# Three buffers for a head's keys and values, two for the padded projections, in a bidirectional gated DeltaNet and GLA layer

## The chip, the cores and the metric

The kernel runs on one core of a Trainium2 chip. The metric is the time of one execution on the device in microseconds (us), median of the runs.

## The reference

One encoder layer on x of 1024 tokens by 1024 channels, in fp32. The input is normalised and goes through one projection; two branches read its columns, and their gated sum goes through an output projection.

```python
h = rmsnorm(x, ln_pre_w)
proj = h @ w_in
...
qkv_a = silu(centred_depthwise_conv(qkv_a, conv_w))          # 5 taps
q_a, k_a = l2norm(q), l2norm(k)                              # 8 heads of 128
o_a = gated_delta_rule(q_a, k_a, v_a, lg_f, beta_f) + flip(gated_delta_rule(flipped, lg_b, beta_b))
y_a = (rmsnorm(o_a, gdn_norm_w) * silu(z_a)) @ w_proj_gdn
y_b = ...                                                    # gated linear attention, 4 heads
merged = sigmoid(gate_a) * y_a + sigmoid(gate_b) * y_b
out = x + rmsnorm(merged @ w_out, ln_post_w)
```

The delta rule is S_t = a_t S_(t-1) (I - b_t k_t k_t^T) + b_t v_t k_t^T, o_t = S_t q_t, for each head and each direction. The reference works by chunks, with a triangular solve in each chunk, and the state goes from chunk to chunk.

## The kernel before

All products of the projections are split: an operand is the sum of two parts of lower precision, and three products of 512 columns (hh·hi, hl·hi, hh·lo) make one of full precision. A projection of 128 output channels (`project`, L256) is 48 products of 512 columns on TensorE (PE), called pj in the rows; its weights come by DMA and are cut into parts by ScalarE (ACT, hi), GpSimd (POOL) or VectorE (DVE, lo).

The delta rule ("GDN") goes head by head, each in three parts that overlap with the neighbours'.

**gdn_project(h)** (L497) makes k, q and v of a head, in this order, and z. Each of k, q, v is projected, evacuated by ACT (L504) into a padded tile xp, whose edges POOL clears (L502), and convolved with five taps over 1024 tokens: the first by DVE (L516; for q by ACT, L514), the others as four `scalar_tensor_tensor` on DVE (L518). The results are the tiles a0 (q), a1 (k), a2 (v), two buffers each, so that head h+1's k takes the place of head h-1's. The four SiLUs of a head (L499), with that of z of the head before, are put together, since ACT loads a table for them and another one to go back (L309, L311).

**gdn_inverse(h)** (L589) works on chunks of 128 tokens, 8 for each direction. PE transposes k (L600), ACT copies it and takes squares (L601, L605) and a logarithm (L613), and makes the decays dt by 16 exponentials (L622). PE multiplies k with itself (L630), DVE makes um of it (L633), and 120 small operations of DVE solve the triangular systems of 32 rows (L655 and L657, tiles tmp and yl). From xq (L665) on, PE and DVE and ACT build larger inverses in turns (L686 to L725), v is transposed and scaled (L733, L734), and q is multiplied with k (L740, L743).

**gdn_scan(h)** (L746) carries the states S of both directions through 8 steps. In each, for both directions: S times k (L781, PE), r (L783, DVE), um times r (L786, PE), vd (L789, DVE) and vn (L791, ACT) from it, kt (ktok times vd, L796, PE), S (L801, DVE) and the outputs po (L770, PE). r reads k by the product and v directly; so the buffers of k and v of head h come free with the end of scan h. After the scan come squares (L816, L817), the norm (L483, L488), and o (L125, L475).

The tile scheduler writes the instruction order of each engine by priorities, the lowest first among what is ready by its own model, which counts the waits for buffers. Scan h (P_HEAD*(h+1)+P_Z) and inverse h (P_HEAD*(h+1)+P_Y) stand ahead of everything with P_FILL: the next head's gdn_project and the gate projections, pj_t (13 of them at head 7), fill what is left. At head 7 stand also `gla_stacks` (L541, tiles r0, r0l), which prepare the second branch.

In `scan_gates` (L401), once at the start, two constant masks are loaded: stl (a tag of its own, 1 KiB in each partition) and mid (tag t2, shared with many small tiles).

Of the kernel before, what the change touches and what calls it, by code (L numbers as in the profile page):

```python
# [8 lines left out]
F32 = mybir.dt.float32  # L9
# [4 lines left out]
P = 128  # L14
T = 1024
# [39 lines left out]
CONSTS = {}  # L55
# [33 lines left out]
def layer_kernel(  # L89
# [6 lines left out]
    nc = tc.nc  # L96
# [16 lines left out]
    @contextmanager  # L113
    def at(priority):

        before = tc.cur_priority
        tc.cur_priority = priority
        yield
        tc.cur_priority = before

    def bank(pool, tag, name):
        return pool.tile([P, 512], F32, tag=tag, name=name)
# [133 lines left out]
    def project(name, evac, src=None):  # L256

        ps = [bank(pj, "pj", f"pj_{name}_{th}") for th in range(2)]
        for g in range(2):
            hi, lo = next_w(name, g)  # L260
            for th in range(2):
                piece(ps[th], hi, lo, src or (hh, hl), th, g, KH)
        for th in range(2):
            evac(th, ps[th])
# [11 lines left out]
    def project_out(name, dst):  # L276


        def evac(th, ps):
            for c in range(2):  # L280
                g_ = gpool.tile([P, 256], F32, tag="gt", name=f"g{name}_{th}_{c}")
                nc.scalar.copy(g_, ps[:, 256 * c:256 * c + 256])  # L282
                nc.sync.dma_start(dst[:, half(th)][:, 256 * c:256 * c + 256], g_)

        project(name, evac)
# [9 lines left out]
    o_c, _ = CONSTS["cf"]  # L295
# [12 lines left out]
    def table(n):  # L308
        tc.keep_in_program_order(nc.scalar.add_instruction(mybir.InstLoadActFuncSet(  # L309
            name=nc.get_next_instruction_name(), engine=mybir.EngineType.Activation, ins=[], outs=[],  # L310
            act_func_set_id=n)))  # L311

    def exp_ln_table():

        table(EXP_LN)
# [85 lines left out]
    def scan_gates(pool):  # L401
# [6 lines left out]
            nc.scalar.dma_start(alog[:, d, :], al.broadcast_to([P, HA]))  # L408
            nc.scalar.dma_start(dtb[:, d, :], dt.broadcast_to([P, HA]))
        smT = pool.tile([64, T], F32, tag="osq", name="smT", bufs=1)  # L410
        stl = pool.tile([P, 2, P], F32, tag="stl", name="stl", bufs=1)
        nc.scalar.dma_start(stl, consts[:, CONSTS["su"][0]:CONSTS["su"][0] + 2 * P].rearrange("p (d i) -> p d i", d=2))
        mid = pool.tile([P, 2, 130], F32, tag="t2", name="mid", bufs=4)
        nc.scalar.dma_start(mid, consts[:, o_c:o_c + 260].rearrange("p (d i) -> p d i", d=2))
        strict = [stl[:, d] for d in range(2)]
        ones = part(tb_, 3, 1)
        nc.gpsimd.memset(ones, 1.0)
        for th in range(2):
# [26 lines left out]
        psg = bank(pg, "g", "psg")  # L445

        for d in range(2):
            rhs = lg[:, d].rearrange("p h n -> p (h n)")
            for q, m in enumerate((mask[d], strict[d], ones)):
                o = (d * 3 + q) * 64  # L450
                nc.tensor.matmul(psg[:, o:o + 64], lhsT=m, rhs=rhs, start=True, stop=True)

            o = 384 + d * 64
            nc.tensor.matmul(psg[:, o:o + 64], lhsT=mid[:, d, :P], rhs=rhs, start=True, stop=True)
        nc.scalar.activation(ev, psg[:, :384].rearrange("p (d q h n) -> p d q h n", d=2, q=3, h=HA), AF.Exp)
        nc.vector.tensor_scalar(nE, ev[:, :, 0], -1.0, None, op0=ALU.mult)
        cm = part(ta_, 0, 1)
# [37 lines left out]
    H64 = (slice(0, 64), slice(64, 128))  # L495

    def gdn_project(h, pool):  # L497
        a = [pool.tile([P, T], F32, tag=f"a{j}", name=f"{'qkv'[j]}{h}", bufs=2) for j in range(3)]
        silu = lambda t: tc.keep_in_program_order(nc.scalar.activation(t, t, AF.Silu))  # L499
        for j in A_ORDER:  # L500
            xp = pool.tile([P, T + 4], F32, tag="xp", name=f"xp{j}_{h}", bufs=XP)
            nc.gpsimd.memset(xp[:, 0:2], 0.0)  # L502
            nc.gpsimd.memset(xp[:, T + 2:T + 4], 0.0)
            evac = lambda th, ps: nc.scalar.copy(xp[:, 2 + th * 512:2 + th * 512 + 512], ps)  # L504
            if h == 0 and j == A_ORDER[0]:
                evac(0, ps_a[0])
                for i in range(2, 4):
                    a_steps[i]()
                evac(1, ps_a[1])
            else:  # L510
                project(f"a{j}_{h}", evac)
            ct = j * 8 + h
            if j == 0:
                nc.scalar.mul(a[j], xp[:, 0:T], cw[:, ct, 0:1])  # L514
            else:
                nc.vector.tensor_scalar(a[j], xp[:, 0:T], cw[:, ct, 0:1], None, op0=ALU.mult)  # L516
            for k in range(1, 5):
                nc.vector.scalar_tensor_tensor(a[j], xp[:, k:k + T], cw[:, ct, k:k + 1], a[j], op0=ALU.mult, op1=ALU.add)  # L518
            if h == 0 and j == A_ORDER[0]:
                table(SILU)  # L520
                silu(a[j])
                exp_ln_table()
        if h == 0:
            table(SILU)
            for j in A_ORDER[1:]:
                silu(a[j])
            exp_ln_table()
            with at(P_FILL):
                project_out("z0", z_d[:, 0])
            return a  # L530
        project_out(f"z{h}", z_d[:, h])
        zs[h - 1] = gdn_z(h - 1, pool)
        table(SILU)
        for t in a + [zs[h - 1]]:
            silu(t)
        exp_ln_table()
        return a
# [33 lines left out]
    def gdn_z(h, pool):  # L571
        z = pool.tile([P, T], F32, tag="zs", name=f"zs{h}", bufs=1)
        nc.sync.dma_start(z, z_d[:, h])
        return z
# [246 lines left out]
    with tc.tile_pool(name="gdn", bufs=1) as pool, tc.tile_pool(name="gdns", bufs=2) as sm:  # L821
        scan_gates(pool)
        o128 = mconst.tile([P, P], F32, name="o128")
        nc.gpsimd.memset(o128, 1.0 / 128)
        with at(P_HEAD):
            dt = gdn_decay(0, pool)
        qkv = gdn_project(0, pool)
        for h in range(HA):
            with at(P_HEAD * (h + 1) + P_Y):
                inv = gdn_inverse(h, pool, sm, qkv, dt)  # L830
            if h < HA - 1:
                with at(P_HEAD * (h + 1) + P_DT):
                    dt = gdn_decay(h + 1, pool)
            cur = qkv
            with at(P_FILL + P_HEAD * (h + 1)):
                if h < HA - 1:
                    qkv = gdn_project(h + 1, pool)
            with at(P_FILL + P_HEAD * (h + 1)):
                gates(("gdn", h))
            if h == HA - 1:  # L840
                with at(P_HEAD * (h + 1) + P_Z - 1000):
                    gla_stacks(pool)
            with at(P_HEAD * (h + 1) + P_Z):
                gdn_scan(h, pool, sm, cur, *inv)
# [311 lines left out]
```

## Time and profile before

| | |
|---|---|
| Median of three runs | 1640.31 us (1637.06 to 1645.77) |
| The profiled execution | 1647.96 us, of it the span 1646.2 us |
| TensorE busy | 1538.3 us, 93% of the span |
| VectorE busy | 871.7 us, 53% |
| ScalarE busy | 704.3 us, 43% |
| GpSimd busy | 190.5 us, 12% |
| Mean granted clock of TensorE | 0.958 of full speed |

The busy times are sums over the whole span. The eight heads of the delta rule take the time from about 40 to 850 us, some 90 us for each; the second branch and the output projection take the rest, in which TensorE is nearly always busy. The clock is the share of the full 2.4 GHz that the chip granted; a dip means stretches at the lower level of 1.2 GHz.

### The profile page before, as it was taken

The numbers are of one execution on the slowest core, as the hardware profiler recorded it, in microseconds if no ns is written. First come the engines' busy times: TensorE is split into PE (matmuls) and PEld (weight loads), VectorE is DVE, ScalarE is ACT, GpSimd is POOL, SyncE is SP. The second block draws the span as 40 slices with busy tenths as digits, with TensorE's granted clock in tenths as the row PEclk, the third lists the DMA queues.
The fourth block names the chain that finished last, engine by engine and source line by source line (L and its number), as shares of the span: only waits on it lengthen the run. The fifth ranks groups of instructions, "written<-read, shape, count | busy, mean of one in ns | idle before, by whom it ended". The sixth has DMA issues, their size and how long they took to land.

```text
span 1646.2 us, 24982 instructions
## 1 busy us (share of the span) xinstructions
PE 1538.3 (93%) x9500; PEld 1295.8 (79%) x9500; DVE 871.7 (53%) x2252; ACT 704.3 (43%) x1488; POOL 190.5 (12%) x207
## 2 busy tenths in 40 slices
PE   6988978998998999899899999999999999999998
PEld 6867866777787878787677888898898988787887
DVE  5485485877879696878531012323314336445413
ACT  5452454436363635554332233535425545423311
POOL 3220111111213011110000020010120100000000
PEclk9996987999898999999999999999999999999999
DMA  5320221131212113131233322131131234755414
GB/s 160 126 68 18 80 71 33 33 106 36 96 46 90 46 33 116 50 99 48 77 121 100 103 65 64 27 103 33 55 85 48 80 100 143 238 157 173 128 45 154
DMA packets 142435, 142.07 MB, mean 86 GB/s; under 512 B 11419, under 2 KB 115403, under 8 KB 141285
## 3 DMA queue, kind: packets, MB, share of 16 engines
q1 hardware_dynamic: 134546, 126.11, 25.6%
q10 hardware_dynamic: 7128, 12.26, 2.4%
q0 software_dynamic: 640, 2.10, 0.4%
q8 instruction: 75, 1.23, 0.3%
q14 instruction: 46, 0.38, 0.1%
HBM read 109.98 MB, written 30.46 MB: 85 GB/s over the span
## 4 chain that ended last, share of the span: by engine, by line
PE 64%; DVE 16%; ACT 11%; DMA 5%; issue 3%; SPq 0%; POOL 0%; ACTq 0%; DVEq 0%; POOLq 0%
PE pj_t L252 8%; PE pj_y L252 7%; PE pj_v L241 6%; PE pout L141 5%; PE pj_g L252 5%; DVE yl L657 4%; PE pj_a L252 4%; DVE tmp L655 4%; PE pj_z L252 4%; PE pj_k L252 3%; PE pj_q L252 2%; ACT dt L622 2%; PE po L770 2%; PE psb L948 2%; PE pob L970 2%
## 5 line engine op out<-in xcount | busy, mean ns | idle before, releaser
L252 PE MATMUL pj_a<-hh,hi_a 128*128 128x512 f32 x368 | 153.6, 417 | 16.5 <-ACT xp L504 9.4
L252 PE MATMUL pj_a<-hl,hi_a 128*128 128x512 f32 x368 | 152.6, 415 | 0.0
L252 PE MATMUL pj_a<-hh,lo_a 128*128 128x512 f32 x368 | 152.1, 413 | 0.0
L252 PE MATMUL pj_t<-hh,hi_t 128*128 128x512 f32 x256 | 103.9, 406 | 2.8 <-ACT gt L282 2.8
L252 PE MATMUL pj_t<-hh,lo_t 128*128 128x512 f32 x256 | 104.2, 407 | 0.0
L252 PE MATMUL pj_t<-hl,hi_t 128*128 128x512 f32 x256 | 103.7, 405 | 0.0
L182 POOL TENSOR_TENSOR lo_a<-raw_a,hi_a 128x512 fp32r<-128x512 f32 x48 | 63.8, 1329 | 311.0 <-ACT hi_a L178 257.0
L252 PEld LDWEIGHTS pj_a<-hh,hi_a 128*128 128x128 f32 x368 | 73.0, 198 | 31.6 <-ACT xp L504 10.2
L657 DVE TENSOR_TENSOR yl<-yl,tmp 128x54 f32<-128x54 f32 (+13 forms) x480 | 96.3, 241 | 0.1
L655 DVE TENSOR_TENSOR tmp<-ulb,yl 128x54 f32<-128x54 f32 (+13 forms) x480 | 90.4, 228 | 0.1
L252 PEld LDWEIGHTS pj_a<-hl,hi_a 128*128 128x128 f32 x368 | 72.4, 197 | 13.9 <-issue 0.7
L252 PEld LDWEIGHTS pj_a<-hh,lo_a 128*128 128x128 f32 x368 | 72.4, 197 | 13.7 <-issue 0.8
L252 PE MATMUL pj_y<-ob,hi_y 128*128 128x512 f32 x256 | 79.1, 390 | 0.9 <-DVE gb L1075 0.9
L141 PE MATMUL pout<-wo,hh 128*128 128x512 f32 (+1 forms) x272 | 79.7, 377 | 0.0
L791 ACT COPY vn<-psc 128x128 f32<-128x128 f32 x128 | 32.2, 265 | 108.5 <-DVE vd L789 72.1
L241 PE MATMUL pj_v<-lo_v,hh 128*128 128x256 f32 x256 | 72.5, 283 | 0.0
L241 PE MATMUL pj_v<-hi_v,hl 128*128 128x256 f32 x256 | 72.5, 283 | 0.0
L241 PE MATMUL pj_v<-hi_v,hh 128*128 128x256 f32 x256 | 72.5, 283 | 0.0
L796 PE MATMUL psc<-vd,ktok 128*128 128x128 f32 x224 | 45.4, 304 | 24.8 <-ACT vn L791 24.7
L182 POOL TENSOR_TENSOR lo_v<-raw_v,hi_v 128x512 fp32r<-128x512 f32 x32 | 41.3, 1290 | 233.1 <-ACT hi_v L178 229.0
L796 PEld LDWEIGHTS psc<-vd,ktok 128*128 128x128 f32 x224 | 34.7, 198 | 39.5 <-ACT vn L791 37.7
L184 DVE TENSOR_TENSOR lo_t<-raw_t,hi_t 128x512 fp32r<-128x512 f32 x32 | 22.0, 689 | 71.7 <-ACT hi_t L178 71.7
(315 smaller groups left out, 4024.2 us busy)
## 6 DMA issues: line engine op xcount, KB each, us to landing
raw_a<-in_w_in_dram SPq DMA_DIRECT2D x48, 256.0 KB
dt<-cr_d SPq DMA_DIRECT2D x8, 1024.0 KB
qe<-eg_d SPq DMA_DIRECT2D x16, 512.0 KB
raw_t<-in_w_in_dram SPq DMA_DIRECT2D x32, 256.0 KB
gt_d<-gt SPq DMA_DIRECT2D x64, 128.0 KB
raw_v<-in_w_in_dram SPq DMA_DIRECT2D x32, 256.0 KB
xt<-in_x_dram SPq DMA_DIRECT2D x8, 512.0 KB
raw_z<-in_w_in_dram SPq DMA_DIRECT2D x16, 256.0 KB
```

The source lines that it names most:

```text
L141: nc.tensor.matmul(ps, lhsT=a(k), rhs=b(k), start=(s == 0), stop=(s == len(steps) - 1))
L182: nc.gpsimd.tensor_tensor(lo, raw, hi.bitcast(F32), op=ALU.subtract)
L241: nc.tensor.matmul(ps[b][:, c * 256:(c + 1) * 256], lhsT=a[th][:, kk, ts], rhs=w[:, k, :], start=kk == 0 and i == 0 and c == 0, stop=kk == ...
L252: nc.tensor.matmul(ps[:, cols], lhsT=a[:, k, :], rhs=b[th][:, kk, cols], start=kk == 0 and a is hi and b is src[0], stop=kk == KD - 1 and ...
L622: nc.scalar.activation(dt[:, u], dt[:, u], AF.Exp, bias=bias[:, d, n:n + 1])
L655: nc.vector.tensor_tensor(tv, ul2[:, i, 0:i].unsqueeze(2).broadcast_to([P, i, w_]), yv[:, i].unsqueeze(1).broadcast_to([P, i, w_]), op=ALU ...
L657: nc.vector.tensor_tensor(yv[:, 0:i], yv[:, 0:i], tv, op=ALU.subtract)
L770: nc.tensor.matmul(po_n(n), lhsT=lhsT, rhs=rhs, start=count[b] == 1, stop=count[b] == len(todo[b]))
L791: nc.scalar.copy(vn[d], pc[d][:, P:2 * P])
L796: nc.tensor.matmul(pc[d][:, 2 * P:3 * P], lhsT=ktok[:, ns], rhs=vd[d], start=True, stop=True)
L948: nc.tensor.matmul(p_s[:, :256], lhsT=ktok[:, u], rhs=vt[:, n], start=True, stop=True)
L970: nc.tensor.matmul(po[e][:, j * P:(j + 1) * P], lhsT=a, rhs=b, start=(i == 0), stop=(i == len(todo) - 1))
```

## The change

The tiles k and v of `gdn_project` get three buffers each, q keeps two (`A_BUFS`, by the index j of q, k, v). The padded tile xp gets two in place of three. To make room, the masks stl and mid become one tile msk of tag t2: stl's own tag is gone, and of mid only the 128 columns that are used are loaded. Nothing that is computed changes. Lines from L37 on stand two, from L417 on one line further down in the changed kernel.

```diff
--- before.py
+++ after.py
@@ -31,7 +31,9 @@
 C_GBT = 8256
 
 
-WRAW, WSPLIT, XS, XP = 2, 4, 4, 3
+WRAW, WSPLIT, XS, XP = 2, 4, 4, 2
+
+A_BUFS = (2, 3, 3)
 
 A_ORDER = (1, 0, 2)
 
@@ -408,11 +410,10 @@
             nc.scalar.dma_start(alog[:, d, :], al.broadcast_to([P, HA]))
             nc.scalar.dma_start(dtb[:, d, :], dt.broadcast_to([P, HA]))
         smT = pool.tile([64, T], F32, tag="osq", name="smT", bufs=1)
-        stl = pool.tile([P, 2, P], F32, tag="stl", name="stl", bufs=1)
-        nc.scalar.dma_start(stl, consts[:, CONSTS["su"][0]:CONSTS["su"][0] + 2 * P].rearrange("p (d i) -> p d i", d=2))
-        mid = pool.tile([P, 2, 130], F32, tag="t2", name="mid", bufs=4)
-        nc.scalar.dma_start(mid, consts[:, o_c:o_c + 260].rearrange("p (d i) -> p d i", d=2))
-        strict = [stl[:, d] for d in range(2)]
+        msk = pool.tile([P, 4, P], F32, tag="t2", name="msk", bufs=4)
+        nc.scalar.dma_start(msk[:, 0:2], consts[:, CONSTS["su"][0]:CONSTS["su"][0] + 2 * P].rearrange("p (d i) -> p d i", d=2))
+        nc.scalar.dma_start(msk[:, 2:4], consts[:, o_c:o_c + 260].rearrange("p (d i) -> p d i", d=2)[:, :, :P])
+        strict, mid = ([msk[:, 2 * q + d] for d in range(2)] for q in range(2))
         ones = part(tb_, 3, 1)
         nc.gpsimd.memset(ones, 1.0)
         for th in range(2):
@@ -451,7 +452,7 @@
                 nc.tensor.matmul(psg[:, o:o + 64], lhsT=m, rhs=rhs, start=True, stop=True)
 
             o = 384 + d * 64
-            nc.tensor.matmul(psg[:, o:o + 64], lhsT=mid[:, d, :P], rhs=rhs, start=True, stop=True)
+            nc.tensor.matmul(psg[:, o:o + 64], lhsT=mid[d], rhs=rhs, start=True, stop=True)
         nc.scalar.activation(ev, psg[:, :384].rearrange("p (d q h n) -> p d q h n", d=2, q=3, h=HA), AF.Exp)
         nc.vector.tensor_scalar(nE, ev[:, :, 0], -1.0, None, op0=ALU.mult)
         cm = part(ta_, 0, 1)
@@ -495,7 +496,7 @@
     H64 = (slice(0, 64), slice(64, 128))
 
     def gdn_project(h, pool):
-        a = [pool.tile([P, T], F32, tag=f"a{j}", name=f"{'qkv'[j]}{h}", bufs=2) for j in range(3)]
+        a = [pool.tile([P, T], F32, tag=f"a{j}", name=f"{'qkv'[j]}{h}", bufs=A_BUFS[j]) for j in range(3)]
         silu = lambda t: tc.keep_in_program_order(nc.scalar.activation(t, t, AF.Silu))
         for j in A_ORDER:
             xp = pool.tile([P, T + 4], F32, tag="xp", name=f"xp{j}_{h}", bufs=XP)
```

The scheduler writes other orders on it. On PE, DVE and ACT they are the same up to the solve of head 2 (487 rows on DVE). Three places follow.

DVE, first tap of head 5's k (`k5`), before; `r3_0_7` and `r3_1_7` are the last r of scan 3, `yl4` and `tmp4` the solve of head 4:

```order
L655 TENSOR_TENSOR tmp4_4_1_5064<-ulb4_4901,yl4_4903 128x28
L655 TENSOR_TENSOR tmp4_2_0_5073<-ulb4_4901,yl4_4903 128x14
L783 SCALAR_TENSOR_TENSOR r3_0_7_4795<-psc3_0_7_4792,nE_533,v3_3317 128x128
L657 TENSOR_TENSOR yl4_4903<-yl4_4903,tmp4_4_1_5064 128x4x7
L657 TENSOR_TENSOR yl4_4903<-yl4_4903,tmp4_2_0_5073 128x2x7
L783 SCALAR_TENSOR_TENSOR r3_1_7_4798<-psc3_1_7_4793,nE_533,v3_3317 128x128
L655 TENSOR_TENSOR tmp4_3_1_5070<-ulb4_4901,yl4_4903 128x24
L655 TENSOR_TENSOR tmp4_1_0_5079<-ulb4_4901,yl4_4903 128x8
L516 TENSOR_SCALAR k5_5272<-xp1_5_5274,cw_110 128x1024
L657 TENSOR_TENSOR yl4_4903<-yl4_4903,tmp4_3_1_5070 128x24
L657 TENSOR_TENSOR yl4_4903<-yl4_4903,tmp4_1_0_5079 128x8
L518 SCALAR_TENSOR_TENSOR k5_5272<-xp1_5_5274,cw_110,k5_5272 128x1024
```

and now, where `vd3_1_2` and `S3_0_2` belong to the third of scan 3's eight steps:

```order
L656 TENSOR_TENSOR tmp4_30_1_4907<-ulb4_4900,yl4_4902 128x30
L656 TENSOR_TENSOR tmp4_28_0_4916<-ulb4_4900,yl4_4902 128x28
L790 TENSOR_SCALAR vd3_1_2_4665<-psc3_1_2_4652,c2_3_3874 128x128
L658 TENSOR_TENSOR yl4_4902<-yl4_4902,tmp4_30_1_4907 128x30
L658 TENSOR_TENSOR yl4_4902<-yl4_4902,tmp4_28_0_4916 128x28
L517 TENSOR_SCALAR k5_5271<-xp1_5_5273,cw_110 128x1024
L656 TENSOR_TENSOR tmp4_29_1_4913<-ulb4_4900,yl4_4902 128x29
L656 TENSOR_TENSOR tmp4_27_0_4922<-ulb4_4900,yl4_4902 128x27
L802 SCALAR_TENSOR_TENSOR S3_0_2_4670<-S3_0_1_4642,ev_532,psc3_0_2_4651 128x128
L658 TENSOR_TENSOR yl4_4902<-yl4_4902,tmp4_29_1_4913 128x29
L658 TENSOR_TENSOR yl4_4902<-yl4_4902,tmp4_27_0_4922 128x27
L802 SCALAR_TENSOR_TENSOR S3_1_2_4673<-S3_1_1_4645,ev_532,psc3_1_2_4652 128x128
```

k5's first tap stood behind scan 3's last r, at the end of head 4's solve; now it stands near that solve's beginning, with the scan at its third step.

DVE, end of head 3's solve, before; `qe` are the decayed q, `k4`, `q4`, `v4` the convolutions of head 4, `xq3` the result on which the first product of L686 waits:

```order
L663 COPY yq3_4111<-ytb3_4109 128x32x16
L752 TENSOR_TENSOR qe0_3_4594<-qe0_3_4594,q3_3315 128x1024
L665 STREAM_TRANSPOSE xq3_4113<-yq3_4111 128x512
L678 COPY xa3_4123<-yq3_4111 32x8x32
L676 COPY xa3_4123<-xq3_4113 32x8x32
L677 COPY xa3_4123<-xq3_4113 32x8x32
L679 COPY xa3_4123<-yq3_4111 32x8x32
L518 SCALAR_TENSOR_TENSOR k4_4294<-xp1_4_4296,cw_110,k4_4294 128x1024
L689 TENSOR_SCALAR p1s3_4162<-p1_3_4129 128x256
L518 SCALAR_TENSOR_TENSOR q4_4293<-xp0_4_4368,cw_110,q4_4293 128x1024
L516 TENSOR_SCALAR v4_4295<-xp2_4_4440,cw_110 128x1024
```

and now:

```order
L753 TENSOR_TENSOR qe1_3_4596<-qe1_3_4596,q3_3314 128x1024
L656 TENSOR_TENSOR tmp3_1_1_4103<-ulb3_3922,yl3_3924 128x8
L519 SCALAR_TENSOR_TENSOR q4_4292<-xp0_4_4367,cw_110,q4_4292 128x1024
L658 TENSOR_TENSOR yl3_3924<-yl3_3924,tmp3_1_1_4103 128x8
L519 SCALAR_TENSOR_TENSOR v4_4294<-xp2_4_4439,cw_110,v4_4294 128x1024
L660 COPY yt3_4106<-yl3_3924 128x512
L519 SCALAR_TENSOR_TENSOR q4_4292<-xp0_4_4367,cw_110,q4_4292 128x1024
L662 STREAM_TRANSPOSE ytb3_4108<-yt3_4106 128x512
L519 SCALAR_TENSOR_TENSOR v4_4294<-xp2_4_4439,cw_110,v4_4294 128x1024
L664 COPY yq3_4110<-ytb3_4108 128x32x16
L519 SCALAR_TENSOR_TENSOR v4_4294<-xp2_4_4439,cw_110,v4_4294 128x1024
L666 STREAM_TRANSPOSE xq3_4112<-yq3_4110 128x512
```

The taps of q4 and v4 and `qe1_3` stood behind `xq3`, now they stand ahead of it.

ACT, opening of head 4's inverse, before; `zs3` is the SiLU of z of head 3, `dt4` are the decays:

```order
L605 ACTIVATE pk4_1_4838,n2_4_4827<-pk4_1_4838 128x128
L791 COPY vn3_0_3_4691<-psc3_0_3_4680 128x128
L791 COPY vn3_1_3_4696<-psc3_1_3_4681 128x128
L613 ACT_TABLE_LOAD
L613 ACTIVATE nk_4_4849<-n2_4_4827 128x8
L499 ACT_TABLE_LOAD
L499 ACTIVATE zs3_4586<-zs3_4586 128x1024
L622 ACT_TABLE_LOAD
L622 ACTIVATE dt4_4285<-dt4_4285,bias_4_4855 128x128 x16
L639 COPY ul4_4890<-um4_4875 32x32x8 x4
```

and now, the SiLUs of head 4 (in the first piece) and the same opening (in the second):

```order
L500 ACTIVATE q4_4292<-q4_4292 128x1024
L500 ACTIVATE k4_4293<-k4_4293 128x1024
L500 ACTIVATE v4_4294<-v4_4294 128x1024
L707 COPY um3_3896<-py_3_4163 32x8x32 x2
L500 ACTIVATE zs3_4585<-zs3_4585 128x1024
L717 ACTIVATE p2s3_4236<-p2_3_4219 128x512
L311 ACT_TABLE_LOAD
```

```order
L606 ACTIVATE pk4_1_4837,n2_4_4826<-pk4_1_4837 128x128
L792 COPY vn3_1_0_4613<-psc3_1_0_4604 128x128
L606 ACTIVATE pk4_1_4837,n2_4_4826<-pk4_1_4837 128x128
L614 ACTIVATE nk_4_4848<-n2_4_4826 128x8
L623 ACTIVATE dt4_4284<-dt4_4284,bias_4_4854 128x128 x16
L640 COPY ul4_4889<-um4_4874 32x32x8 x4
L792 COPY vn3_0_1_4634<-psc3_0_1_4623 128x128
L792 COPY vn3_1_1_4639<-psc3_1_1_4624 128x128
```

The SiLU of zs3 left the place between the logarithm of L613 and the exponentials and now stands behind those of q4, k4 and v4, and the three table loads around it are gone from there.

## Rows read from the trace of the kernel before

**Rows 1.** Timeline of PE; columns: start, us, instruction, tiles, shape, count, [idle before, releaser].
```profile
393.31 0.71 PE L796 MATMUL psc<-vd,ktok 128*128 128x128 f32 x4 [1.63 <-ACT vn L791]
...
432.63 1.02 PE L686 MATMUL p<-xq,um 32*32 32x32 f32 x29 [1.54 <-DVE xq L665]
```

**Rows 2.** Windows, PK to A, head 4 and sum: length, busy by engine, granted clock, DMA.
```profile
468.80:486.10 17.30, 16.07 (x100) 13.86 (x100) 8.98 (x24) 17.17 (x49) 0.00 (x0) 1.00 0.01 2
...
sum 86.00, PE 75.09 PEld 64.12 DVE 42.19 ACT 84.61 POOL 0.38; mean PE 15.02 PEld 12.82 DVE 8.44 ACT 16.92 POOL 0.08
```

**Rows 3.** The same view, A to P1: head 3, sum of heads 3 to 7.
```profile
393.30:432.60 39.30, 33.49 (x164) 26.29 (x164) 38.09 (x154) 17.88 (x32) 11.05 (x8) 1.00 0.24 78
...
sum 184.60, PE 165.70 PEld 134.70 DVE 175.68 ACT 69.44 POOL 42.53; mean PE 33.14 PEld 26.94 DVE 35.14 ACT 13.89 POOL 8.51
```

**Rows 4.** The same view, P1 to the next PK: head 3, head 7, sum.
```profile
432.60:468.80 36.20, 36.16 (x353) 30.63 (x354) 25.15 (x41) 11.81 (x27) 4.72 (x10) 0.81 0.27 84
...
784.00:849.60 65.60, 56.41 (x485) 46.32 (x485) 32.53 (x75) 24.25 (x54) 2.08 (x4) 0.92 0.27 85
sum 202.70, PE 193.01 PEld 162.03 DVE 134.95 ACT 77.10 POOL 19.57; mean PE 38.60 PEld 32.41 DVE 26.99 ACT 15.42 POOL 3.91
```

**Rows 5.** The same view, the tail behind scan 7.
```profile
849.60:955.00 105.40, 102.63 (x447) 84.49 (x447) 14.40 (x20) 25.20 (x61) 2.75 (x4) 0.98 0.38 108
```

**Rows 6.** Timeline of DVE at the end of scan 3.
```profile
512.72 0.35 DVE L783 SCALAR_TENSOR_TENSOR r<-psc,nE,v 128x128 f32<-128x128 f32 x1 [1.69 <-PE psc L781]
512.99 0.25 DVE L655 TENSOR_TENSOR tmp<-ulb,yl 128x24 f32<-128x24 f32 x2
513.15 0.75 DVE L516 TENSOR_SCALAR k<-xp,cw 128x1024 f32<-128x1024 f32 x1
```

**Rows 7.** Timeline of PE: products of 512 columns; 16 of 128 columns.
```profile
1252.14 0.39 PE L252 MATMUL pj_q<-hh,hi_q 128*128 128x512 f32 x1
...
1253.29 0.39 PE L252 MATMUL pj_q<-hh,lo_q 128*128 128x512 f32 x1
...
205.34 2.05 PE L630 MATMUL pgr<-k 128*128 128x128 f32 x16
```

**Rows 8.** DVE: L518 (ns min/median/max), then groups by form (busy us, mean ns).
```profile
L518 DVE SCALAR_TENSOR_TENSOR k<-xp,cw,k x32: 1266/1274/2342, 55.5 to 710.3; 128x1024 f32<-128x1024 f32 x32
...
L752 DVE TENSOR_TENSOR qe<-qe,q 128x1024 f32<-128x1024 f32 x10 | 12.1, 1214 | 0.0
...
L817 DVE TENSOR_TENSOR osq<-osq,o 128x512 f32<-128x512 f32 x12 | 8.2, 687 | 7.9 <-ACT o L816 7.8
...
L475 DVE SCALAR_TENSOR_TENSOR o<-po,gdn_w,zs 128x512 f32<-128x512 f32 x10 | 7.2, 733 | 0.0
...
L125 DVE TENSOR_TENSOR zs<-osq,zs 128x1024 f32<-128x1024 f32 x5 | 6.6, 1319 | 0.0
```

**Rows 9.** Timeline of ACT in head 4's opening, and the group of L504.
```profile
473.30 1.28 ACT L613 ACT_TABLE_LOAD   x1
...
476.11 1.06 ACT L499 ACTIVATE zs<-zs 128x1024 f32<-128x1024 f32 x1
477.18 1.28 ACT L622 ACT_TABLE_LOAD   x1
478.47 4.80 ACT L622 ACTIVATE dt<-dt,bias 128x128 f32<-128x128 f32 x16
...
L504 ACT COPY xp<-pj_a 128x512 f32<-128x512 f32 x24 | 13.8, 588 | 11.4 <-PE pj_a L252 11.3
```

**Rows 10.** Timelines of PE and DVE in scan 7.
```profile
820.91 0.80 PE L786 MATMUL psc<-r,um 128*128 128x128 f32 x2 [5.80 <-DVE r L783]
...
819.91 0.68 DVE L165 TENSOR_TENSOR r0l<-r,r0h 64x512 fp32r<-64x512 f32 x1 [5.57 <-ACT r0h L164]
```

**Rows 11.** Waits of PE, 376.3 to 849.6 us; columns: total, times, longest.
```profile
PE psc L796 <- ACT vn L791: 20.8, 15, 3.4
```

**Rows 12.** Timeline of PE, head 3's k-q product.
```profile
454.49 1.95 PE L740 MATMUL pkq<-q,k 128*128 128x128 f32 x16
```

## The prediction

> **What bounds the kernel now.** I read the page first: TensorE (PE) is busy nearly all the span, and the chain of work that ended last is mostly PE. Such a share is an average, so I cut the stretch that the change can move, 376.3 to 849.6 us (heads 3 to 7 of the delta rule, "GDN"), at instructions that return in each head, found in the timeline of PE [rows 1]: **PK**, the first transpose of k at L600, which opens an inverse; **A**, the first kt product (L796) after the 16 decay exponentials of L622; and **P1**, the first product on the solve's result (L686). The windows view then gives busy time by stretch.
>
> PK to A is ScalarE's (ACT): 84.61 us busy of 86.00 over five heads, PE 75.09 [rows 2]. A to P1 is VectorE's (DVE): 175.68 of 184.60, PE 165.70 [rows 3]; here stand the 120 small operations of the solve, and whatever else is queued among them. P1 to the next PK is PE's: 36.16 of 36.20 in head 3, and over all five heads what is missing is almost only the last, where 56.41 of 65.60 are busy [rows 4]. The tail to 955 is PE's as well, 102.63 of 105.40 [rows 5].
>
> Now the wait that the change is about. With two buffers k5's convolution can't start before the last read of k3, in scan 3. In the timeline of DVE it starts (L516) 0.43 us after that scan's last r [rows 6]; the order puts k3, k4, k6 and k7 just so at the end of scans 1, 2, 4, 5. But the neighbours of rows 6 show no gap: the engine goes from one to the next, because the scheduler has written that wait into the order. So no wait on DVE comes free; what changes is **which operations stand in which stretch**, and a stretch costs what its own bound engine costs.
>
> **The change part by part.** Order and counts are from the two instruction orders; durations from the trace.
>
> 1. *Up to head 2's solve* both orders are the same (487 rows of DVE). From there to head 3's PK stand 2 scan operations (0.35 each [rows 6]) and one L516 (0.75 [rows 6]) more on DVE, 1.4, and some 12 products of 512 columns more on PE. One such takes 0.23 from start to start (five in 1252.14 to 1253.29 [rows 7]): 2.7. The two lie beside each other and PE is the full one: **+2.7**.
>
> 2. *A to P1, on DVE.* Third buffers let the taps of k, and behind them those of q and v, move up into the solve. Costs: a tap (L518) 1.27, qe (L752) 1.21, osq (L817) 0.69, zs (L125) 1.32, o (L475) 0.73 [rows 8], a scan operation 0.35 and an L516 0.75 [rows 6]. Head 3: 7 taps, one L516 and one L752 more, 6 scan operations less, 8.9+0.8+1.2-2.1 = +8.8. Head 4: one tap less, 9 scan operations more, two L817, one L125, one L475 less, -1.3+3.2-1.4-1.3-0.7 = -1.5. Head 5: three taps, two L817, one L125, one L475 more, three scan operations less, 3.8+1.4+1.3+0.7-1.0 = +6.2. Head 6: six scan operations more, L125 and L475 less, 0. Head 7: four less, two L817 more, 0. Sum **+13.5**. DVE has 8.9 us idle in these stretches (184.60 less 175.68), which could swallow part: I take none, since it is idle where the scan's products make it wait, and keep half (4.5) for the range.
>
>    DVE collides here: a tap takes 1.27 alone but up to 2.34 [rows 8], and the long ones lie beside a GpSimd (POOL) operation. The Trainium skill, "SBUF — State Buffer", section "Who interferes with whom", says that a DVE operation with two inputs in SBUF and a POOL operation that reads SBUF exclude each other, which the trace bears out. By POOL's share of head 3's stretch, 11.05 of 39.3 [rows 3], the added 8.8 would cost 8.8 x 0.28 = 2.5 more. I leave it out, as POOL's operations stay as many, and put 2.5 at the upper end.
>
> 3. *What PE gets done meanwhile.* The work of PE is the same in all, so what it does earlier is missing later. In A to P1 the filling projections count 96, 101, 83, 100, 73 products before and 149, 86, 104, 90, 73 now. With the scan's 128-wide products at 0.26 (16 passes, that is 8 products, in 2.05 [rows 7]): head 3 +53 x 0.23 = 12.2 less ten scan products, 2.6; head 4 -3.5+1.7; head 5 +4.8+1.1; head 6 -2.3+2.6; head 7 +0.4. Sum +14.4. PK to A loses 0.8. With the 2.7 of step 1, 16.3 us of products leave the PE-bound stretches, 5.4 of it from the gate projections in the tail (432 products in its last run before, 408 now). There PE is full, so they end **16.3** earlier. This is the term on which the forecast hangs; if these stretches weren't PE's, it is nothing (rival C).
>
> 4. *PK to A of head 4.* In the order of ACT the SiLU of zs3 stood between the inverse's Ln and its exponentials, with three table loads of 1.28 around them, the first at 473.30, the last at 477.18 [rows 9]. It now stands with the SiLUs of q4, k4, v4 before PK; the load of L613 goes too. Three loads at 1.28 and the SiLU at 1.06 leave the ACT-bound stretch, one evacuation of xp (L504, 0.59 [rows 9]) enters: 3.84+1.06-0.59 = **-4.3**.
>
> 5. *Scan 7.* The only long wait of the last scan is 5.80 us at 820.91: its r stands on DVE behind r0l (L165), a piece of the GLA stacks that waited for a transfer [rows 10]. In the new order r0l stands two operations later, behind that r, and head 6's finish ahead of it. What the r then waits for isn't shown: it may still wait for the scan's own chain, so between 0 and -5.8. No row is nearer to one end than to the other, so I take somewhat less than the middle, since a new neighbour can't be excluded: **-2.5**.
>
> 6. *Two buffers for xp.* v's evacuation of the next head must wait for the k taps of the same head; in head 3, summing the order by the same prices, PE is through with the next projection's products about 2 us before the taps are, so 0 to +2.2, beside a stretch that is DVE's. Taken at nothing; if it shows on PE, +2.2. The masks come by two transfers as before, on the same queue, the second a little smaller, in the opening where the order of the others is unchanged: nothing.
>
> Sum: 2.7+13.5-4.3-16.3-2.5 = **-6.9 us**. The profiled execution took 1647.96 us (span 1646.2), the median of the three runs is 1640.31; the difference carries over: 1633.4. Bounds of this sum: high, 2.5 (collisions), 2.2 (xp) and 2.5 (scan 7 as before) more, +0.3; low, 4.5 (idle of DVE) and 3.3 (scan 7) less, -14.7.
>
> **The rivals.**
>
> *A. The sum,* 1626 to 1641, likeliest 1633.4.
>
> *B. Bubbles close.* PE's gap before kt returns in every head: 15 waits, 20.8 us [rows 11]. If later scan steps fall out of PK to A, since they now stand among the solve, no kt is left there to wait, and the gaps go: 1640.3-20.8 = 1619.5. In the Trainium skill, "Perfetto Trace Analysis", section "Optimization Strategy", a gap that repeats on the engine that should be full can mean too few buffers, which this change adds. Against it: the gap ends with ACT's copy of vn, which stands behind the 16 exponentials, 4.80 us [rows 9]; no buffer is named there, and in the new order kt still stands behind them in each head.
>
> *C. The added DVE work stays, the gain doesn't come.* P1 to PK holds a chain of its own: from P1 at 432.63 [rows 1] to the k-q product of L740 at 454.49 [rows 12] it takes 21.9 us in head 3, alternating between engines. If the chain and not PE's fill sets its length once products have left it, steps 1, 2 and 4 stand and 16.3 is lost: 2.7+13.5-4.3 = +11.9, 1652. It decides from the point where PE idles in that stretch. Against it, PE has 36.16 of 36.20 and the chain is 14 us shorter than the stretch, 12 of which the change takes; for it, that only 2 us are then left, and that PE's granted clock was 0.81 there [rows 4], so that fewer products may come at a better clock and leave PE idle the sooner.
>
> *D. Nothing moves.* The wait was never PE's; PE is busy, the reordered pieces cancel: 1640.
>
> **How the numbers follow.** Chances: A 0.60, B 0.15, C 0.15, D 0.10. What can be told from no change is some 0.5%, 8.2 us, so faster is below 1632.1 and slower above 1648.5. A lies across the first: I give 0.27 of its 0.60 to faster and 0.33 to same. Faster 0.27+0.15 = 0.42, same 0.33+0.10 = 0.43, slower 0.15. The range takes in A, B and D and leaves out C (0.15): from B's 1619 to 1646, which is D with the spread of the three runs (highest 1645.77). A alone has 1626 to 1641.
>
> **What would show it.** Right: head 3's A to P1 is longer by 7 to 11 us, with its DVE as full as before, and the next P1 to PK shorter by about 12; head 4's PK to A is some 13 us with no SiLU in it; the wait at scan 7's r is gone or halved; the kt waits are about as long as before. Wrong, if PE shows idle time in P1 to PK of heads 3 to 6 (C), if the kt waits sum to a few us (B), if a v evacuation (L504) waits for taps and PE behind it for over 2 us (step 6), or if taps get a median well above 1.3 us (step 2).

## The result

The changed kernel is faster by 0.65%: the ratio of its runs to those of the kernel before is 0.9935, with a 95% interval of 0.9913 to 0.9957. Its median is 1633.24 us of 18 runs, that of the kernel before, run beside it, 1644.74 us. By the ratio that is 10.7 us less; the forecast had 6.9 less. The profiled execution of the changed kernel took 1628.58 us. It lies below its set's median, as the one of before (1647.96) lies above its own, so the two profiles differ by more than the medians do. (One of the 18 runs was disturbed and is in neither the ratio nor the table below.)

From the page of the changed kernel: the span, TensorE's line of part 1, and the granted clock in 40 slices.

```profile
span 1626.8 us, 25004 instructions
...
PE 1523.7 (94%) x9500; PEld 1280.4 (79%) x9500; DVE 875.4 (54%) x2252; ACT 699.2 (43%) x1484; POOL 187.3 (12%) x207
...
PEclk9986987999999999999999999999999999999999
```

The span is 19.4 us shorter, and TensorE's busy time fell by 14.6 (from 1538.3), with the same 9500 instructions. Only the rest, 4.8 us, is idle time that went. The same work in less busy time means that it ran faster: the mean granted clock of the two profiled executions is 0.958 and 0.969.

Windows of the changed kernel (length, then busy us of each engine with its instructions, granted clock, DMA). PK to A, head 4 and the sum of heads 3 to 7, against [rows 2]:

```profile
463.50:476.80 13.30, 12.18 (x74) 10.05 (x73) 8.26 (x23) 11.98 (x44) 0.00 (x0) 1.00 0.02 7
...
sum 82.80, PE 74.21 PEld 63.52 DVE 44.28 ACT 80.70 POOL 0.00; mean PE 14.84 PEld 12.70 DVE 8.86 ACT 16.14 POOL 0.00
```

A to P1, head 3 and the sum, against [rows 3]:

```profile
391.00:443.60 52.60, 44.17 (x198) 34.24 (x199) 50.24 (x157) 17.87 (x33) 13.26 (x14) 0.97 0.31 100
...
sum 197.10, PE 176.80 PEld 141.59 DVE 190.25 ACT 68.43 POOL 41.27; mean PE 35.36 PEld 28.32 DVE 38.05 ACT 13.69 POOL 8.25
```

P1 to the next PK, heads 3 to 7 and the sum, against [rows 4]:

```profile
443.60:463.50 19.90, 19.90 (x279) 16.53 (x279) 7.74 (x16) 12.09 (x19) 3.19 (x5) 0.91 0.17 50
512.50:553.20 40.70, 38.83 (x381) 32.40 (x381) 32.41 (x53) 16.50 (x36) 6.64 (x9) 0.92 0.31 106
611.90:638.10 26.20, 26.20 (x323) 22.60 (x324) 20.86 (x34) 11.01 (x25) 4.39 (x8) 1.00 0.38 118
692.60:723.10 30.50, 29.74 (x341) 25.43 (x340) 27.11 (x40) 14.07 (x28) 2.74 (x3) 1.00 0.32 103
771.10:835.60 64.50, 56.88 (x497) 46.73 (x497) 31.46 (x71) 22.80 (x51) 2.08 (x4) 0.97 0.29 90
sum 181.80, PE 171.54 PEld 143.69 DVE 119.59 ACT 76.47 POOL 19.05; mean PE 34.31 PEld 28.74 DVE 23.92 ACT 15.29 POOL 3.81
```

So the picture of the forecast is there: the solve's stretch is longer (by 12.5 us), ScalarE's is shorter (3.2), TensorE's is shorter (20.9). But the column of the clock changed as well. In [rows 4] it read 0.81 in head 3; it reads 0.91 now, and 1.00 in heads 5 and 6.

The three heads of before that [rows 4] leaves out, 4 to 6:

```profile
526.80:558.30 31.50, 31.48 (x328) 26.56 (x328) 22.93 (x35) 11.70 (x24) 5.35 (x10) 0.84 0.29 90
611.30:651.90 40.60, 40.17 (x390) 34.17 (x391) 30.28 (x52) 17.60 (x35) 6.86 (x12) 0.92 0.35 118
706.90:735.70 28.80, 28.78 (x329) 24.36 (x329) 24.06 (x39) 11.75 (x24) 0.56 (x1) 0.94 0.33 102
```

What the clock takes can be priced. A stretch of length L at a mean clock c did L x c of full-speed work, so L x (1-c) was lost to the lower level, 1.2 GHz. In P1 to PK that is 22.1 us before (clocks 0.81, 0.84, 0.92, 0.94, 0.92 in the five heads) and 7.0 now: **15.1 of the 20.9 us are the clock's.** The forecast had no term for that. (Where TensorE waits at the lower level, the price counts that time too, so it is an upper one; here TensorE is busy in 193.01 of 202.70 us before and in 171.54 of 181.80 now.)

### The profile page after: what moved, and what is told of

Read it like the earlier page. It is cut to its first block, busy times and chain, and to the rows that moved or that the text cites. A ratio compares the mean times of both kernels' runs of the same rounds, so it can differ in the third digit from the quotient of the medians.

```text
span 1626.8 us, 25004 instructions
## 1 busy us (share of the span) xinstructions
PE 1523.7 (94%) x9500; PEld 1280.4 (79%) x9500; DVE 875.4 (54%) x2252; ACT 699.2 (43%) x1484; POOL 187.3 (12%) x207
## 4 chain that ended last, share of the span: by engine, by line
PE 47%; ACT 6%; DVE 5%; DMA 5%; issue 1%; SPq 1%; DVEq 0%; ACTq 0%
PE pj_t L254 7%; PE pj_y L254 7%; PE pj_v L243 6%; PE pout L143 5%; PE pj_g L254 5%; PE pj_k L254 3%; PE pj_q L254 2%; PE psb L949 2%; PE pob L971 1%; DVE tmp L656 1%; DVE yl L658 1%; PE pj_z L254 1%; PE pc L903 1%; PE pa L934 1%; DMA st<-ob_d 1%
## 5 line engine op out<-in xcount | busy, mean ns | idle before, releaser
L254 PEld LDWEIGHTS pj_a<-hh,hi_a 128*128 128x128 f32 x368 | 72.7, 197 | 31.7 <-ACT xp L505 10.3
L254 PEld LDWEIGHTS pj_a<-hl,hi_a 128*128 128x128 f32 x368 | 72.4, 197 | 13.5 <-issue 0.5
L254 PEld LDWEIGHTS pj_t<-hh,hi_t 128*128 128x128 f32 x256 | 48.6, 190 | 13.4 <-ACT gt L284 4.0
```

The lines of the kernel that those rows point to most:

```text
L254: nc.tensor.matmul(ps[:, cols], lhsT=a[:, k, :], rhs=b[th][:, kk, cols], start=kk == 0 and a is hi and b is src[0], stop=kk == KD - 1 and ...
```

## The experiments

Each kernel ran beside the kernel before on one chip. The line "before" pools the 39 runs beside e1 to e10; for the 18 beside the changed kernel, whose mean is 1643.2 us, no clock was kept. The table gives the mean of all runs, the mean granted clock, and the span taken apart by it as above: span times clock, and what was lost to the lower level, each with its standard error. The split is over a whole run, so it doesn't depend on a choice of profile.

| Kernel | runs | us | clock | span x clock | lost |
|---|---|---|---|---|---|
| before | 39 | 1644.2 | 0.960 | 1576.4 ± 0.4 | 66.0 ± 1.0 |
| changed | 17 | 1632.5 | 0.966 | 1574.6 ± 0.7 | 56.1 ± 1.3 |
| e1, k and v two buffers | 12 | 1644.5 | 0.959 | 1576.0 ± 0.5 | 66.7 ± 1.8 |
| e2, third k, three xp | 5 | 1626.8 | 0.968 | 1573.5 ± 0.9 | 51.4 ± 2.1 |
| e3, changed, z's SiLU first | 5 | 1622.9 | 0.966 | 1565.2 ± 0.5 | 55.8 ± 1.5 |
| e4, changed, v's tap on ScalarE | 4 | 1609.6 | 0.976 | 1568.8 ± 0.9 | 39.0 ± 0.4 |
| e5, before, dense products among the small | 6 | 1684.6 | 0.947 | 1592.8 ± 1.2 | 90.0 ± 3.0 |
| e6, before, small products twice | 6 | 1703.3 | 0.938 | 1596.6 ± 1.0 | 104.9 ± 1.5 |
| e7, before, v's tap on ScalarE | 6 | 1624.2 | 0.966 | 1567.5 ± 1.1 | 54.9 ± 2.9 |
| e8, everything that paid | 6 | 1595.8 | 0.976 | 1555.7 ± 1.1 | 38.3 ± 1.3 |
| e9, before, no small products | 5 | 1589.2 | 0.975 | 1548.4 ± 1.5 | 39.1 ± 1.7 |
| e10, changed, no small products | 6 | 1591.6 | 0.979 | 1555.9 ± 0.9 | 33.9 ± 1.0 |

By the first two lines the change is worth 1.8 us (± 0.8) of work and waiting and 9.9 (± 1.6) of clock.

**Which part of the change does it.** Two orders answer half of that without a run. With three buffers for k alone (two for v) the instruction orders of all engines are the same, row for row, as those of the changed kernel: the third buffer of v does nothing. With the merged masks alone the orders of VectorE, GpSimd and the DMA queue are those of before, and those of TensorE and ScalarE differ only in the name of the mask, in six rows of the opening. The runs took the rest.

e1, the changed kernel with its buffers undone:

```diff
-A_BUFS = (2, 3, 3)
+A_BUFS = (2, 2, 2)
```

> The changed kernel with two buffers for k and v again (the two xp buffers and the merged masks stay). Theory 1 (the third buffer of k is what pays): the convolutions wait for the scan's end again, the gain is gone, within 3 us of the kernel before. Theory 2 (the sum of the prediction: what pays is which operations stand in which stretch, whatever put them there): the order alone gives, by the prices of the prediction, +5.9 in the solves, -4.3 for one table visit less, -8.1 of products out of PE's stretches, together about -6.5 us against before, nearly as much as the full change. Theory 3 (the gain is the clock's): the time at an equal granted clock is that of before within 4 us, and the rest of the difference goes with the clock of the run.

Measured: 0.9992 of before (0.9969 to 1.0015). Theory 1 stands: without the third buffer of k nothing is gained. Theory 3 holds too: at an equal clock the kernel is 0.4 us from before. Theory 2 falls here: it had -6.5 us, and the interval ends near -5. The order did change, from the end of head 3's solve on, and by the prices of the prediction it should have paid; it didn't, and the clock stayed at that of before. The two stretches where the changed order hits hardest, A to P1 of head 4 and what follows P1:

```profile
487.80:540.60 52.80, 42.38 (x188) 33.25 (x188) 52.03 (x151) 19.85 (x33) 17.61 (x17) 0.97 0.36 110
...
540.60:567.90 27.30, 27.25 (x274) 23.35 (x275) 6.78 (x15) 9.58 (x17) 1.77 (x2) 0.55 0.07 21
```

The second is short of products, as step 3 says, but nearly all of it ran at the lower level (0.55). Just before it TensorE had waited 4.7 us for the solve's result.

e2, the third buffer of k by itself, with xp as before:

```diff
-WRAW, WSPLIT, XS, XP = 2, 4, 4, 2
-A_BUFS = (2, 3, 3)
+WRAW, WSPLIT, XS, XP = 2, 4, 4, 3
+A_BUFS = (2, 3, 2)
```

> Three buffers for k alone, three for xp as before, the masks merged (which alone leaves the order of before). Theory 1: as the changed kernel, about -10 us against before. Theory 2: by the same prices +11.2 in the solves, -4.3, -9.3 of products and 0 to -2.5 in scan 7: about -2 to -5 us. Theory 3: at an equal granted clock within 4 us of before.

Measured: 0.9888 (0.9867 to 0.9909), which is 17 us under before and 5.7 under the changed kernel. So two xp buffers in place of three cost, again mostly in the clock (4.7 of the 5.7, with an error of 2.5); they do so beside the third k buffer, while with two for k the same step cost nothing (e1). Theory 1 had about 10 us in all, theory 2 had 2 to 5. Theory 3 comes nearest: at span times clock the kernel is 2.9 us under before, within its 4, and the rest is the clock.

**What the clock answers to.** In the trace the longest stretch at the lower level begins, in heads 3 to 6 of the kernel before, 0.8, 2.2, 3.0 and 6.4 us after P1. In heads 3 to 5 that is while the 160 small products of 32 rows and 32 columns run (L686, L695, L701; the trace counts two passes for each product, so they are 80 products of the code), in head 6 0.9 us after the last of them. In head 7 no such stretch begins there. Four experiments turn on that.

e6, these products twice:

```diff
-                    nc.tensor.matmul(p1[B32(e), n * 32:n * 32 + 32], ...)
+                    for _ in range(2):
+                        nc.tensor.matmul(p1[B32(e), n * 32:n * 32 + 32], ...)
(the same for py)
```

> The kernel before, with each of the small products of L686 and L695 made twice (the same result): 1024 products of 32 columns more, about 0.026 us each at full clock, 27 us if all of it stands in TensorE's way. Clock theory: the clock falls below 0.955 and the time lost to the lower level grows from 67 us to 75 or more. Rival: it stays at 67 within 3, and the time grows by the products alone.

e5, a dense product behind each 16 small ones:

```diff
+                nc.tensor.matmul(p1[:, 256:512], lhsT=hh[0][:, 0, 0:P], rhs=hh[0][:, 0, 0:256],
+                                 start=True, stop=True)
(the same for py)
```

> The kernel before, with one product of 256 columns, whose result is not read, behind each 16 of the small 32-row products of L686 and L695: 64 more in all, some 0.11 us each at full clock, 7 us. Clock theory (the granted clock falls where the inverse's small products run, and dense products among them hold it up): the mean clock of the runs rises from 0.959 to 0.963 or more, the time lost to the lower level falls from 67 us by 7 or more, and the time stays within 4 us of before. Rival (the small products have nothing to do with it): clock as before within its spread, time +7 us; the scheduler moves other work too, which can shift either by some us.

e9, the kernel before without the small products:

```diff
-        for d in range(2):
-            for a, e in pairs[d]: ...     (64 passes for p1)
+        for d in range(2):
+            nc.tensor.matmul(p1[:, d * P:(d + 1) * P], lhsT=ident,
+                             rhs=xsrc(d)[:, 0:4].rearrange("p u i -> p (u i)"), start=True, stop=True)
(py and px: one product each with the identity)
```

> The kernel before, with the 160 small 32-row products of L686, L695 and L701 in each head replaced by four dense ones with the identity (the inverse is then not built: that part of the computation is left out). The small ones take 4.5 us a head at full clock and 7.3 at half [burst from P1 to the last px], so the work falls by some 30 us. Clock theory: with the bursts gone the time lost to the lower level falls from 66 us by 20 or more. Rival (something else in these stretches lowers the clock): it stays at 66 within 5.

e10, the same in the changed kernel:

> The same in the changed kernel. Clock theory, if the bursts were what before and after differ by: the two kernels without bursts lose the same time to the lower clock, and differ by no more than 3 us in all. Rival (the third buffer of k acts by work and waits): this one stays 10 us or more ahead.

Here are 20 us from P1 on, by windows: the kernel before (heads 3, 4, 7), the changed kernel (3, 4, 6), e6 (3, 7), e5 (3), e9 (3, 6), e10 (3, 5). The third column from the end is the granted clock.

```profile
432.60:452.60 20.00, 19.96 (x250) 16.89 (x251) 12.29 (x17) 4.65 (x10) 1.41 (x3) 0.66 0.25 86
526.80:546.80 20.00, 20.00 (x258) 16.67 (x259) 13.77 (x19) 5.88 (x13) 2.71 (x6) 0.74 0.29 93
...
784.00:804.00 20.00, 19.89 (x287) 16.46 (x287) 11.98 (x23) 10.59 (x22) 1.03 (x2) 1.00 0.17 52
```

```profile
443.60:463.60 20.00, 20.00 (x280) 16.62 (x281) 7.84 (x16) 12.09 (x19) 3.19 (x5) 0.91 0.18 51
512.50:532.50 20.00, 19.89 (x281) 17.54 (x281) 12.95 (x26) 6.49 (x17) 0.14 (x2) 0.83 0.02 6
...
692.60:712.60 20.00, 19.30 (x284) 16.71 (x284) 17.27 (x24) 8.37 (x16) 2.74 (x3) 1.00 0.41 131
```

```profile
455.40:475.40 20.00, 19.99 (x328) 17.89 (x329) 11.30 (x17) 3.90 (x9) 2.05 (x5) 0.57 0.28 94
...
836.40:856.40 20.00, 20.00 (x338) 17.72 (x338) 7.83 (x14) 6.88 (x13) 1.03 (x2) 0.66 0.20 58
```

```profile
444.00:464.00 20.00, 19.87 (x195) 15.75 (x196) 11.48 (x17) 4.01 (x10) 2.06 (x5) 0.57 0.28 93
```

```profile
411.30:431.30 20.00, 19.83 (x152) 16.73 (x153) 18.38 (x30) 7.11 (x17) 2.97 (x6) 1.00 0.36 119
...
659.00:679.00 20.00, 19.92 (x148) 15.89 (x148) 18.16 (x29) 10.91 (x22) 4.66 (x3) 1.00 0.32 120
```

```profile
415.80:435.80 20.00, 19.88 (x150) 16.79 (x150) 16.93 (x25) 11.64 (x24) 3.76 (x7) 0.93 0.30 91
...
586.10:606.10 20.00, 19.96 (x148) 16.75 (x149) 16.95 (x25) 11.47 (x24) 3.75 (x7) 0.92 0.32 100
```

TensorE is busy in all of them, and the clock is not the same. With the small products twice it is 0.57 to 0.66 in each of heads 3 to 7; without them it is 1.00 in all five of e9. Over the whole run the lost time is 104.9 us, 66.0 and 39.1, in this order. So in the kernel before, more of the small products lower the clock in these stretches, and leaving them out raises it: that much is shown. They are not enough by themselves, since the changed kernel has 1.00 in heads 5 to 7 with them, and they are not the only cause, since e10 has 0.93 and 0.92 in heads 3 and 5 without them.

e5 went the other way than the clock theory had it: the dense products didn't hold the clock up, 90.0 us were lost. The rival, with the clock as before, falls as well. By the starts in the timeline the group from the first of L686 to the last of L701 became longer, from 5.5 to 9.5 us in heads 3 to 7 to 10.3 to 14.7. A longer group lost more, as in e6; but a lower clock makes the group longer too, and that the length is the reason was not tried apart.

e9 and e10 are the test of the change itself. Without the small products the change brings nothing: the ratios are 0.9676 (0.9646 to 0.9705) and 0.9687 (0.9658 to 0.9717), the means 2.4 us (± 1.3) apart, the changed one behind. So the rival, 10 us ahead, falls. But of what the clock theory expected only the equal time came: the changed one still loses 5.2 us (± 2.0) less to the clock and has 7.5 (± 1.7) more of work and waiting, where with the small products it had 1.8 less. In all four kernels the scheduler also puts other work elsewhere, so these sums hold more than the small products, and the pair doesn't show that the dips at the small products are the whole of the gain.

What stands directly before P1 goes with the dips as well. From head 3's PK to scan 7's end, the waits of TensorE for the solve's result (total, times, longest), before and now:

```profile
PE p L686 <- DVE xq L665: 5.3, 4, 2.1
```

```profile
PE p L687 <- DVE xq L666: 3.5, 2, 2.2
```

They stand in heads 3 to 6 before and in heads 3 and 5 now. In the traces of the eight kernels that have the small products as they were (before, changed, e1 to e4, e7, e8), heads 2 to 7, TensorE is idle for more than 0.3 us directly before P1 in 18 of 48 cases. A stretch at the lower level begins, from 4 us before P1 to 8 us behind it, in 16 of these 18, and in 8 of the other 30. This fits the third k buffer, with which TensorE has more products to do during the solve (502 against 453 in step 3). It is not a proof: the changed kernel's head 5 has the wait and no dip, its head 4 the dip and no wait, and no run changed the wait alone.

**Steps 2 and 4, each pushed further.** e3 takes the SiLU of z out of the opening of all inverses:

```diff
-        for t in a + [zs[h - 1]]:
+        for t in [zs[h - 1]] + a:
```

> The changed kernel with the SiLU of the earlier head's z put ahead of those of q, k and v in each head, so that it leaves the stretch between the inverse's logarithm and its exponentials in heads 5 to 7 and 2 too; 8 table loads less than the changed kernel. Theory 2, step 4: each such stretch about 3.6 to 4.3 us shorter, in all -10 us against the changed kernel. Rival: PE is about 90% busy in these stretches, so its products only move into stretches that are PE's, and what is gained is at most the idle time of PE there, some 8 us in all heads, likely 2 to 4 us. Theory 3: the clock decides, no more than 3 us at an equal clock.

Measured: 0.9858 (0.9838 to 0.9878), 9.6 us under the changed kernel, all of it in span times clock (9.4). Theory 2's 10 us came; theory 3, with no more than 3 us at an equal clock, misses here. The opening of head 5 and the sum:

```profile
554.20:569.30 15.10, 13.90 (x92) 12.13 (x90) 9.03 (x25) 14.98 (x47) 0.00 (x0) 1.00 0.01 2
...
sum 73.90, PE 68.40 PEld 59.75 DVE 45.42 ACT 72.24 POOL 0.00; mean PE 13.68 PEld 11.95 DVE 9.08 ACT 14.45 POOL 0.00
```

Each opening that still had the SiLU in it is 2.0 to 2.5 us shorter, not 3.6 to 4.3, since two of the three table loads stay in its place. The sum over the five heads is 8.9 us less. That is more than the 2 to 4 us that the rival held likely, and about the 8 that it gave as the most.

e4 moves a tap of v to ScalarE in the changed kernel, e7 in the kernel before:

```diff
-            if j == 0:
+            if j != 1:
                 nc.scalar.mul(a[j], xp[:, 0:T], cw[:, ct, 0:1])
```

> The changed kernel with the first tap of v on ScalarE, as that of q is, in place of VectorE. Theory 2 (A to P1 is VectorE's): 0.74 us less on VectorE in each head where it stands in the solve, at most -5 us, if the order stayed; the order changes too (by the prices +4 in the solves of the first two heads). Rival: ScalarE in P1 to PK and PK to A is later for it, 1.1 us a head, 0 to +5 us.

> The kernel before with the first tap of v on ScalarE and nothing else. If the gain of the v tap is VectorE's relief in the solve (0.74 us a head) and the earlier start of heads 0 and 1, it comes without the third buffer of k too: 20 us or more under before. If it needs the third buffer: 10 us or less. Clock theory: most of the gain stands in the granted clock, above 0.965.

Measured: 0.9777 (0.9757 to 0.9797) and 0.9886 (0.9843 to 0.9929). The 5 us that VectorE's relief could give were far too little, and the rival's loss didn't come. e7 is 20 us under before, so the tap pays without the third k buffer too; 11.1 of the 20 are the clock's, and with 0.966 that theory is met, if narrowly. Most of the gain of e4 against the changed kernel is the clock's (17.1 of 22.9 us), a good part of it in heads 0 and 1. From the first PK to the third, the kernel before (the changed one has a clock of 0.84 in both) and e4:

```profile
81.40:201.50 120.10, 106.22 (x685) 88.19 (x683) 78.37 (x221) 48.93 (x111) 22.17 (x26) 0.86 0.19 57
201.50:285.40 83.90, 67.76 (x474) 56.07 (x475) 57.74 (x173) 42.29 (x86) 11.54 (x15) 0.84 0.19 54
```

```profile
81.30:177.60 96.30, 87.51 (x613) 73.03 (x612) 73.09 (x202) 43.22 (x100) 20.17 (x24) 0.91 0.20 56
177.60:269.40 91.80, 80.20 (x558) 65.77 (x558) 66.51 (x188) 47.55 (x97) 18.57 (x19) 0.91 0.22 70
```

By these clocks 30 us were lost there before and 17 in e4; TensorE's instructions move from the first stretch to the second. That the freed VectorE is what moves them was not tried apart.

e7 and e4 differ by the change that this document is about, and are its second measurement: 14.6 us, of which span times clock has -1.3 (± 1.4) and the lost time 15.9 (± 2.9). Again the change acts through the clock. (The two ran on different chips; the kernel before beside them differed by 2.3 us, 1.5 of it lost to the clock.)

e8 puts together what paid:

```diff
 (the changed kernel with the lines of e2, e3 and e4)
```

> The changed kernel with two buffers for v and three for xp, the SiLU of z first, and v's first tap on ScalarE: everything that paid alone. If the gains add, 1632.5 less 5.7 less 9.6 less 22.9, 1594 us. Rival: they take the same idle time and the same dips of the clock from each other, and the time stays at 1605 to 1610 as with the v tap alone.

Measured: 0.9716 (0.9679 to 0.9752), median 1596.85 us, the quickest of these kernels that computes the whole layer: 2.8% under before. The gains add: the mean of 1595.8 (± 1.7) agrees with the 1594 of the sum.

## Why the prediction came out near, and where it was wrong

The predicted 1633.4 lies near the measured time, for half of the reasons. Step by step, from the two profiled executions:

- *Step 1, up to head 3's PK, +2.7.* From head 2's PK to head 3's it was 90.9 us and is 90.3; without what the clock lost (1.7 before, nothing now) that is 1.1 more. The term was small and is smaller. Its count was wrong, its price right by luck: up to that point TensorE does 5 products of 512 columns fewer, not 12 more, and 15 of the scan's more, which is 2.8 by the prediction's prices.
- *Step 2, A to P1, +13.5.* The sum is right: 184.6 to 197.1, +12.5, with VectorE as full as before (190.25 of it). In it two misses offset each other. Head 3 took more than its +8.8, namely 13.3, outside the 7 to 11 of the prediction's sign. POOL's operations there went from 8 to 14, 13.26 us; the same 120 operations of the solve took 27.3 us against 23.9, and one tap 2.32, and that tap and the 8 of those 120 that took over 0.7 us (4 before) all lie beside an operation of POOL. So the collisions that were left out had a part in it. Head 4 gave 5.0 back, not 1.5.
- *Step 3, TensorE's stretches and the tail, -16.3.* **This step is the one that was mis-sized.** P1 to PK is 20.9 us shorter, 15.1 of it the clock's, so 5.8 by products. The tail gave what it should, 5.4:

```profile
849.60:1646.20 796.60, 781.64 (x4120) 662.23 (x4119) 266.58 (x451) 303.40 (x589) 52.57 (x46) 1.00 0.35 101
```

```profile
835.60:1626.80 791.20, 776.75 (x4096) 657.51 (x4094) 265.82 (x450) 302.83 (x586) 52.56 (x46) 1.00 0.34 101
```

  Together 11.2 at an equal clock, against 16.3 and the 2.5 of step 5. Part of it is the count: TensorE has 24 products of 512 columns fewer in the tail, and in P1 to PK 12 such and 24 of the scan's fewer, which is 14.5 by the prediction's prices.
- *Step 4, head 4's opening, -4.3.* Right: 17.3 to 13.3, -4.0. In ScalarE's timeline the exponentials follow the logarithm with no table load between:

```profile
468.71 0.21 ACT L614 ACTIVATE nk<-n 128x8 f32<-128x8 f32 x1 [0.24 <-DVE n L609]
469.20 4.79 ACT L623 ACTIVATE dt<-dt,bias 128x128 f32<-128x128 f32 x16 [0.28 <-DVE bias L616]
```

- *Step 5, scan 7, -2.5.* Wrong: the stall moved by one operation. r0l stands behind r now, as the order said, but vd stands behind r0l. Timelines of PE, ACT and DVE there:

```profile
807.48 0.80 PE L797 MATMUL psc<-vd,ktok 128*128 128x128 f32 x2 [4.12 <-ACT vn L792]
...
805.48 0.62 ACT L166 CAST r0h<-r 64x512 fp32r<-64x512 f32 x1 [5.92 <-DMA r<-r_d]
...
806.13 0.68 DVE L167 TENSOR_TENSOR r0l<-r,r0h 64x512 fp32r<-64x512 f32 x1 [4.71 <-ACT r0h L166]
806.74 0.34 DVE L790 TENSOR_SCALAR vd<-psc,c 128x128 f32<-128x128 f32 x1
```

  VectorE waits 4.71 us for a transfer's sake, and TensorE 4.12 for the vd behind it, where it waited 5.80 for r [rows 10]. Head 7's stretch is 1.1 us shorter, not 2.5, and by the price above the clock gave about 3 there (0.92 to 0.97), so the new order itself gained nothing.
- *Step 6, xp.* Small in the profile, as taken (2.0 us below), but e2 shows that the two buffers cost 5.7 us in the runs beside the third k buffer, mostly by the clock.

Waits of TensorE from head 3's PK to scan 7's end, in the changed kernel:

```profile
PE psc L797 <- ACT vn L792: 19.3, 13, 4.1
PE pm_a L484 <- DVE osq L818: 5.0, 3, 4.1
...
PE pj_z L254 <- ACT xp L505: 2.0, 2, 1.0
```

Rival B is out: the kt waits are 19.3 us, where [rows 11] has 20.8 (4.1 of the 19.3 is the one in scan 7). Rival C is out, but not without a trace: TensorE idles 10.3 us in P1 to PK, 9.7 before, and in heads 3 to 6, which the prediction named as C's sign, 2.6 against 0.5. The wait for osq has grown from 0.6: at its longest, 4.1 us, the finish of head 2 stands behind operations of head 3's solve on VectorE.

What the forecast could not hold is the whole: at an equal clock the runs show -1.8 us (error 0.8) where its sum says -6.9, and the missing gain was made good, and more, by 9.9 us of clock (error 1.6). The number was near because two errors had opposite signs. That 1633.4 meets the median of 1633.24 so closely is luck besides: the forecast started from 1640.31, the median of three runs of before, and the 18 runs beside the changed kernel have 1644.74. Rival C named the clock of 0.81, but as a reason for a loss; it should have been a term of the sum, with a sign of its own.

What stays open: why the third k buffer shortens the dips. The 160 small products are the same, and so is their place in the chain; what stands around them differs, the wait before P1 among it. No run here changed that alone.

## What to carry to other kernels

Where a profile shows TensorE full at a granted clock well under 1, take the span apart as clock times length before summing instructions: a reordering that removes no work can still move the time through the clock, and by more than the work it moves. A buffer that lets work start earlier is first of all a new order; read what now stands behind the operation that waits for a transfer, since its stall can pass to the next one, as the 5.80 us of r became 4.12 of vd here. And measure each part of a bundled change apart: here one buffer paid, one did nothing, and the one given up for them cost beside the one that paid, though alone it had cost nothing.

## What the runs showed of the hardware

That TensorE full of instructions need not keep the full clock. In the kernel before 19.96 of the 20 us from head 3's P1 on are busy, at a clock of 0.66. The same run of 29 small products takes 1.54 us there, at the lower level, and 0.98 in the changed kernel's head 4, before its dip:

```profile
433.61 1.54 PE L686 MATMUL p<-yq,um 32*32 32x32 f32 x29
```

```profile
513.46 0.98 PE L687 MATMUL p<-yq,um 32*32 32x32 f32 x29
```

Also that the clock accounts for most of the spread between runs of one kernel: of the 17 of the changed kernel, the quickest (1621.43) had 0.972, the slowest (1638.68) 0.959, while span times clock stays within 1568 to 1578.
